# The mixture-of-experts part of a diffusion trunk: another order for the program of experts with 97 to 160 tokens

## The chip, the cores and the metric

The kernel runs on one core of a Trainium2 chip. The core has a matrix engine (PE; PEld is its loading of stationary weights), a vector engine (DVE), a scalar engine (ACT), a general engine (POOL) and an engine that only starts transfers (SP); sixteen DMA engines move data between the main memory and the core. Each engine runs its own queue of instructions in order, and they wait for each other by semaphores. The metric is the device time of one execution in microseconds; several runs are taken and their median is given.

## What is computed

One layer of a trunk: a mixing part (projections, convolutions, two recurrent scans) and then a mixture of 32 experts over 256 tokens of width 1024. The change touches the experts alone. Cut to these, the reference is:

```python
def moe_ffn(h, w_router, b_router, w_gate, b_gate, w_up, b_up, w_down, b_down):
    t = h.reshape(-1, shape[-1])                      # 256 x 1024
    logits = t @ w_router + b_router
    top_logit, top_idx = lax.top_k(logits, 4)         # 4 of 32 experts for each token
    top_w = softmax(top_logit)
    combine = ...                                     # expert x token, zero where not chosen
    def expert(acc, prm):
        gate = minimum(t @ wg + bg, 7)
        up = clip(t @ wu + bu, -7, 7)
        y = ((up + 1) * gate * sigmoid(1.702 * gate)) @ wd + bd
        return acc + cw[:, None] * y, None
```

All is float32. The three weight matrices of an expert have 4 MB each, so 384 MB are read in all.

## The kernel before

**Routing.** The number of tokens of each expert is known only when the kernel runs. For each expert the kernel holds five programs and branches to one by the count: up to 32 tokens (the light one), up to 64, up to 96, up to 160, and more. Every program is a list of groups (`SIZES`): a group is a start and a width in the expert's list of tokens. The program for 97 to 160 has three groups: 32 wide from 0, 64 wide from 32, 64 wide from 96. The five programs stand in the code once for each of the 32 experts.

**Gather and one-hots.** `pick` builds a one-hot matrix, tokens by places of the list, by comparing each token's rank in the expert with the place (DVE or POOL). `gather` multiplies the tokens' rows by it on PE, into the bank `xb`, and ACT copies them out. The first 96 places of an expert are gathered ahead, during the expert before; places from 96 on are gathered at the start of its own program. `to_slots` turns a one-hot by two transposes on PE, also into `xb`, and ACT copies it to SBUF (`ST`, `STm`): the turned form is needed to scatter.

**Products.** The weights of an expert are twelve tiles of 1 MB: four for gate, four for up, four for down. `some(prod, i, j)` multiplies group j by tile i: the tokens are PE's stationary operand, the weights stream. A 32-wide group uses a quarter of the columns of the array, so that four parts of the output are computed side by side; a 64-wide one uses a half. The result lies in one PSUM bank (`bk`): two single banks `g0` and `g1` and four banks of one tile `four`. ACT copies it out (`copy`), PE turns it (`fold`, into the bank `fb`), and DVE and ACT make the gate from it (`gated`) or the hidden activation (`up`). `copy` targets are `sA`, `sB`, `sC` and here also `gts[3]`; `gts[j]` holds the gate of group j.

**The ring.** The weights lie in a ring of 16 places of 1 MB. When the last group of an expert has used tile i, `fetch` issues the load of the tile 16 further on, on SP's queue. The loads wait for their place to come free.

**Scatter.** `scatter` multiplies the turned one-hot with the down product of a group (`spread`, into all of `four`) and DVE adds the result, weighted, to `acc` in two instructions (`rows` in the profile). The program of two groups spreads both groups in one accumulation and adds once.

**The order.** The schedule is written out by hand: each engine gets its instructions in the order of the source. For three groups the branch `else` of `program` is taken before the change: gather of the last group; all gate products; copy and gate of each group in turn; all up products; then turning of the first one-hot, copy and fold of each group; gather of the first half of the next expert's tokens; down products; gather of the second half; and for each group by itself a turned one-hot and a scatter. Groups 1 and 2 share the copy target `sC` there.

Of the kernel before, what the change touches and what calls it, by code (L numbers as in the profile page):

```python
# [198 lines left out]
def trunk(ctx: ExitStack, tc: tile.TileContext, I, out, offs, dbg=None, nexp=NE):  # L199
    nc = tc.nc  # L200
    V, S_, P_, G_ = nc.vector, nc.scalar, nc.tensor, nc.gpsimd
# [37 lines left out]
    def t512(name, dt=F32):  # L239
        return tp.tile([128, 512], dt, tag="f2", name=name)  # L240
# [1391 lines left out]
    rs, nb = rn[:, 0:2], rn[:, 2:4]  # L1632
# [83 lines left out]
    def etile(name, *shape):  # L1716
        return ep.tile([128, *shape], F32, name=name)
# [5 lines left out]
    Xm = [etile(f"Xm{i}", n) for i, n in enumerate((512, 512, 256))]  # L1723
    SMm, ST, STm = etile("SMm", 2, 128), etile("ST", T), etile("STm", T)
    gts = [t512(f"gt{i}") for i in range(4)] + [etile("gt4", 256)]
    sA, sB = (etile(n, 512) for n in ("sA", "sB"))
    scr = st.tile([128, 2, 512], F32, tag="hl", name="scr")
    sC, sg = scr[:, 0], scr[:, 1]
# [16 lines left out]
    def gather(Sm, X, n, ks=range(8)):  # L1745

        for k in ks:
            o = (k - ks[0]) * n
            for t in range(2):
                P_.matmul(xb[:, o:o + n], hl[:, t, k * 128:(k + 1) * 128], Sm[:, t, 0:n],  # L1750
                          start=(k == ks[0] and t == 0), stop=(t == 1), skip_group_check=True)
        S_.activation(X[:, ks[0] * n:(ks[-1] + 1) * n], xb[:, 0:len(ks) * n], AF.Copy)  # L1752

    def to_slots(Sm, st_, half=0):

        o = 256 * half
        for t in range(2):
            P_.transpose(xb[:, o + t * 128:o + (t + 1) * 128], Sm[:, t], ident)  # L1758
        S_.activation(st_, xb[:, o:o + 256], AF.Copy)

    def product(ps, e, i, x, n):

        w = raw(e, i)
        m = 8 * n
        for kk in range(2):
            k = 2 * (i % 4) + kk
            for q in range(128 // n):
                P_.matmul(ps[n * q:n * q + n, 0:m], x(k), w[:, kk * 1024 + q * m:kk * 1024 + (q + 1) * m],  # L1768
                          start=(k == 0), stop=(k == 7), skip_group_check=True)
# [5 lines left out]
    def chs(ap, n):  # L1775

        return ap.rearrange("p (c q s) -> p c q s", c=n // 16, s=n)
# [29 lines left out]
    def spread(parts):  # L1807

        for j, (st_, Y, n) in enumerate(parts):
            for t in range(2):  # L1810
                for i in range(n // 32):
                    for q in range(128 // n):
                        b = n // 32 * q + i
                        P_.matmul(four[:, b, t * 256:(t + 1) * 256], st_[n * q:n * q + n, t * 128:(t + 1) * 128],  # L1814
                                  Y[n * q:n * q + n, i * 256:(i + 1) * 256], start=(not j and not t), stop=(j == len(parts) - 1),
                                  skip_group_check=True)
        return [four[:, :, t * 256:(t + 1) * 256] for t in range(2)]

    def scatter(e, parts):

        ps = spread(parts)
        for t in range(2):
            a = acc[:, t].rearrange("p (q m) -> p q m", m=256)
            V.scalar_tensor_tensor(a, ps[t], cw[:, t, e:e + 1], a, op0=OP.mult, op1=OP.add)  # L1824

    def program(e, groups, first=True):

        nb, nxt = len(groups), e + 1 < nexp
        X0, Xn = Xt[e % 2], Xt[1 - e % 2]
        mine = range(0 if first else 1, nb)  # L1830
        ns = [n for a, n in groups]

        Hs = ([X0[:, 0:8 * ns[0]], X0[:, 256:768]] + Xm)[:nb]

        def x(j):
            a, n = groups[j]
            if a < 96:
                X = X0.rearrange("p (k s) -> p k s", s=96)
                return lambda k: X[:, k, a:a + n]
            X = Hs[j].rearrange("p (k s) -> p k s", s=n)  # L1840
            return lambda k: X[:, k]

        def bk(prod, j):
            return banks[(prod * nb + j) % 6]

        def v(ap, j):
            return chs(ap[:, 0:8 * ns[j]], ns[j])

        def some(prod, i, j):
            n = ns[j]  # L1850
            product(bk(prod, j), e, i, hid(v(Hs[j], j), n) if prod == 2 else x(j), n)
            if j == nb - 1:
                fetch(12 * e + i + NP)

        def gated(j, s):
            gate(e, fold(s, ns[j]), ns[j], v(gts[j], j), v(sg, j))

        def up(j, s):
            hidden(e, fold(s, ns[j]), ns[j], v(gts[j], j), v(Hs[j], j))

        def copy(prod, j, s):
            return copied(bk(prod, j), s, ns[j])

        def onehot(j):
            a, n = groups[j]
            return Sq[e % 2] if (a, n) == (0, 32) else pick(e, a, n, 128 // n, SMm, V)

        hint(e + 1)
        if nb == 1:
            for i in range(4):  # L1870
                some(0, i, 0)
            copy(0, 0, sA)
            for i in range(4, 7):
                some(1, i, 0)
            gated(0, sA)
            some(1, 7, 0)
            copy(1, 0, sB)
            if first:
                to_slots(onehot(0), ST)
            up(0, sB)  # L1880
        elif nb == 2:
            Sm = onehot(1)
            for j, s in enumerate((sA, sC)):
                for i in range(4):
                    some(0, i, j)
                copy(0, j, s)
            gated(0, sA)
            for i in range(4, 8):
                some(1, i, 0)
            copy(1, 0, sB)  # L1890
            gated(1, sC)
            for i in range(4, 8):
                some(1, i, 1)
            copy(1, 1, sC)
            up(0, sB)
            if first:
                to_slots(onehot(0), ST)
            to_slots(Sm, STm, 1)
            up(1, sC)
        else:  # L1900
            for j in range(2, nb):
                gather(onehot(j), Hs[j], ns[j])
            for j in range(nb):
                for i in range(4):
                    some(0, i, j)
            for j in range(nb):
                copy(0, j, sC if j else sA)
                gated(j, sC if j else sA)
            for j in range(nb):
                for i in range(4, 8):  # L1910
                    some(1, i, j)
            if first:
                to_slots(onehot(0), ST)
            for j in range(nb):
                copy(1, j, sC if j else sB)
                up(j, sC if j else sB)
        if nxt:
            gather(Sg[1 - e % 2], Xn, 96, range(4))
        if not mine:
            return  # L1920
        if nb == 1:
            for i in range(8, 12):
                some(2, i, 0)
        else:
            for j in mine:
                for i in range(8, 12):
                    some(2, i, j)
        parts = []
        for j, y in zip(mine, (sA, sB, sC, sg, gts[0])):
            parts.append((j, copy(2, j, y), ns[j]))  # L1930
        if nxt:
            gather(Sg[1 - e % 2], Xn, 96, range(4, 8))
        if nb <= 2:
            scatter(e, [(STm if j else ST, y, n) for j, y, n in parts])
        else:
            for j, y, n in parts:
                if j:
                    to_slots(onehot(j), STm)
                scatter(e, [(STm if j else ST, y, n)])
# [111 lines left out]
    for t in range(2):  # L2051
        V.tensor_tensor(xres[:, t], xres[:, t], rows[:, 0], op=OP.mult)
        V.tensor_tensor(xres[:, t], xres[:, t], rows[:, 1], op=OP.add)
    G_.memset(acc, 0.0)
    for e in range(nexp):
        last = e == nexp - 1
        if not last:
            known(e + 1)
            picked(e + 1, G_)
        else:  # L2060
            to_slots(Sq[e % 2], ST)
        if e in (20, 21):
            next(bd_)
        with tc.If(which[e] > 32, label=f"heavy{e}") as light:
            with tc.If(which[e] <= 64) as more:
                program(e, SIZES[2 if last else 3], not last)
            with more.Else():
                with tc.If(which[e] <= 96) as more:
                    program(e, SIZES[2], not last)
                with more.Else():  # L2070
                    with tc.If(which[e] <= 160) as more:
                        program(e, SIZES[1], not last)
                    with more.Else():
                        program(e, SIZES[0], not last)
        with light.Else():
            program(e, SIZES[4], not last)
# [28 lines left out]
```

## Time and profile before

| | |
|---|---|
| median of 3 runs | 1443.89 us (1442.87 to 1446.61) |
| profiled execution | 1443.94 us |
| its span, first to last instruction | 1442.0 us |
| PE busy | 1150.8 us (80%) |
| DVE, ACT, POOL busy | 489.6, 297.6, 192.5 us |
| read from main memory | 456.45 MB, 317 GB/s over the span |

Times of rows are microseconds from the start of the span. A row of the timeline is a run of like instructions on one engine: when it starts, how long it lasts, the line, what it writes and reads, how many; in brackets how long the engine stood idle before it and what ended that. "issue" is idle time for which the profile shows no wait. A float32 product is two instructions on PE. [...]

### The profile page before, as it was taken

What the parts mean: (1) busy time and instruction counts of PE and PEld (TensorE: products, weight loads), DVE (VectorE), ACT (ScalarE), POOL (GpSimd) and SP (SyncE); (2) the same over time, 40 slices, a digit from 0 to 9 for tenths busy, and PEclk for the clock granted to TensorE, in tenths of its full rate; (3) what the DMA queues carried; (4) which work ended last, traced back from release to release, by engine and by line L of the source; (5) the groups of instructions that cost most, each with busy time, mean ns of one, the idle gap of its engine ahead of it and who ended that gap; (6) DMA issues with size and microseconds to landing.
All of it is one profiled execution on the core that took longest, in us unless ns stands there. A gap on an engine that the chain in (4) does not pass through costs nothing.

```text
span 1442.0 us, 26141 instructions
## 1 busy us (share of the span) xinstructions
PE 1150.8 (80%) x11226; PEld 708.8 (49%) x11226; DVE 489.6 (34%) x863; ACT 297.6 (21%) x576; POOL 192.5 (13%) x229
## 2 busy tenths in 40 slices
PE   6797999899697897787787988686677869767783
PEld 1576888678444544354333643353333434433342
DVE  3767767979511211212022211121121112211116
ACT  3456644444210111111010101010001001101012
POOL 0242243450200100010000100010000101000002
PEclk9998979999698998998797989898879989898997
DMA  7634334418796998999943999999999999999970
GB/s 286 239 110 131 111 117 148 175 67 317 317 419 262 417 420 357 418 416 417 385 159 129 412 419 418 417 418 416 419 412 419 408 408 420 405 417 418 416 287 30
DMA packets 129059, 460.59 MB, mean 319 GB/s; under 512 B 9488, under 2 KB 19088, under 8 KB 128048
## 3 DMA queue, kind: packets, MB, share of 16 engines
q1 hardware_dynamic: 128816, 457.52, 79.8%
q8 instruction: 131, 2.15, 0.6%
q14 instruction: 112, 0.92, 0.2%
HBM read 456.45 MB, written 1.05 MB: 317 GB/s over the span
## 4 chain that ended last, share of the span: by engine, by line
PE 54%; DMA 22%; DVE 11%; issue 8%; ACT 4%; SPq 1%; DVEq 0%; ACTq 0%
PE g L1768 18%; PE four L1768 11%; DMA ring<-in_w_down 11%; DMA ring<-in_w_up 6%; PE xb L1750 6%; PE four L1814 3%; DMA ring<-in_w_gate 2%; PE fb L1786 2%; DMA bd<-in_b_down 1%; DMA uada<-in_w_ada 1%; PE psada L429 1%; DVE gt L1794 1%; PE psW L1005 1%; ACT scr L1796 1%; SPq L266 1%
## 5 line engine op out<-in xcount | busy, mean ns | idle before, releaser
L1768 PE MATMUL g<-ring,X 128*32 128x256 f32 (+1 forms) x3680 | 355.9, 472 | 142.2 <-issue 87.5
L1768 PEld LDWEIGHTS g<-ring,X 128*32 128x32 f32 (+1 forms) x3680 | 157.2, 128 | 320.2 <-issue 233.8
L1768 PE MATMUL four<-ring,X 128*32 128x256 f32 (+1 forms) x2272 | 208.6, 435 | 20.3 <-DMA ring<-in_w_down 19.6
L1824 DVE SCALAR_TENSOR_TENSOR rows<-four,cw,rows 128x1024 f32<-128x1024 f32 x66 | 81.7, 1280 | 329.6 <-PE four L1814 329.6
L1794 DVE TENSOR_TENSOR gt<-fb,vc 128x256 f32<-128x256 f32 (+1 forms) x37 | 18.7, 504 | 423.7 <-PE fb L1786 423.7
L1768 PEld LDWEIGHTS four<-ring,X 128*32 128x32 f32 (+1 forms) x2272 | 86.0, 118 | 123.5 <-issue 60.9
L1750 PE MATMUL xb<-Sg,hl 128*128 128x96 f32 x1024 | 135.4, 288 | 4.5 <-DVE Sg L1736 2.6
L1750 PEld LDWEIGHTS xb<-Sg,hl 128*128 128x128 f32 x1024 | 125.6, 200 | 27.2 <-issue 24.6
L1736 POOL TENSOR_SCALAR Sq<-slots,rank 128x128 f32<-128x128 f32 x62 | 39.4, 647 | 580.8 <-PE xb L1758 342.2
L1772 ACT ACTIVATE sA<-g 128x256 f32<-128x256 f32 (+1 forms) x33 | 14.0, 423 | 342.5 <-PE g L1768 342.5
L645 POOL TENSOR_TENSOR adas<-adas,uada 128x1024 f32<-128x1024 f32 x24 | 59.8, 2492 | 99.3 <-ACT uada L643 98.9
L1736 POOL TENSOR_SCALAR Sg<-slots,rank 128x96 f32<-128x96 f32 x62 | 31.6, 521 | 301.1 <-PE xb L1750 257.3
L1752 ACT ACTIVATE X<-xb 128x384 f32<-128x384 f32 x64 | 31.4, 491 | 123.4 <-PE xb L1750 117.9
L1796 ACT ACTIVATE scr<-gt 128x256 f32<-128x256 f32 (+1 forms) x37 | 17.7, 480 | 172.8 <-DVE gt L1795 172.8
L1772 ACT ACTIVATE sA<-four 128x256 f32<-128x256 f32 (+1 forms) x30 | 12.8, 427 | 163.1 <-PE four L1768 163.1
L1814 PE MATMUL four<-sA,ST 32*128 32x256 f32 (+1 forms) x512 | 42.7, 406 | 1.6 <-DVE sA L1985 1.6
L643 ACT ACTIVATE uada<-uada,sT 128x1024 f32<-128x1024 f32 x32 | 35.7, 1140 | 9.4 <-DMA uada<-in_w_ada 9.2
L1802 DVE TENSOR_TENSOR X<-fb,vc 128x256 f32<-128x256 f32 (+1 forms) x36 | 18.0, 499 | 54.2 <-PE fb L1786 54.2
L1005 PEld LDWEIGHTS <-before 64*64 64x64 f16 x1088 | 29.8, 115 | 9.8 <-issue 3.8
L1814 PEld LDWEIGHTS four<-sA,ST 32*128 32x128 f32 (+1 forms) x512 | 28.1, 188 | 6.5 <-DVE sA L1985 2.1
L1797 DVE TENSOR_TENSOR gt<-gt,scr 128x256 f32<-128x256 f32 (+1 forms) x37 | 18.9, 510 | 20.5 <-ACT scr L1796 20.5
L1768 PE MATMUL four<-ring,Xm 128*64 128x512 f32 x96 | 21.1, 592 | 0.0
(560 smaller groups left out, 1558.0 us busy)
## 6 DMA issues: line engine op xcount, KB each, us to landing
ring<-in_w_gate SPq DMA_DIRECT2D x128, 1024.0 KB, 18.1
ring<-in_w_up SPq DMA_DIRECT2D x128, 1024.0 KB, 17.8
ring<-in_w_down SPq DMA_DIRECT2D x128, 1024.0 KB, 18.1
uada<-in_w_ada SPq DMA_DIRECT2D x24, 1024.0 KB, 5.3
uout<-in_w_out SPq DMA_DIRECT2D x4, 1024.0 KB, 5.2
uE<-in_w_in SPq DMA_DIRECT2D x2, 1024.0 KB, 5.5
uF<-in_w_in SPq DMA_DIRECT2D x4, 512.0 KB, 4.0
uG<-in_w_in SPq DMA_DIRECT2D x2, 1024.0 KB, 5.3
```

What stands on the lines that cost most here:

```text
L643: S_.activation(u[:, kk], u[:, kk], AF.Copy, scale=sT3[:, 2 * h + kk, 0:1])
L645: G_.tensor_tensor(acc_, acc_, u[:, kk], op=OP.add)
L1005: P_.matmul(ps[cs, x * 64:x * 64 + 64], L[cs, x], R[cs, x] if len(R.shape) == 3 else R[cs], start=True, stop=True, skip_group_check=True)
L1736: eng.tensor_scalar(Sm[:, t, 0:m * n].rearrange("p (q s) -> p q s", s=n), slots[:, a:a + n].unsqueeze(1).to_broadcast([128, m, n]), rank[: ...
L1750: P_.matmul(xb[:, o:o + n], hl[:, t, k * 128:(k + 1) * 128], Sm[:, t, 0:n], start=(k == ks[0] and t == 0), stop=(t == 1), skip_group_check ...
L1752: S_.activation(X[:, ks[0] * n:(ks[-1] + 1) * n], xb[:, 0:len(ks) * n], AF.Copy)
L1768: P_.matmul(ps[n * q:n * q + n, 0:m], x(k), w[:, kk * 1024 + q * m:kk * 1024 + (q + 1) * m], start=(k == 0), stop=(k == 7), skip_group_che ...
L1786: P_.transpose(fb[:, c * 128:(c + 1) * 128], s[:, c * 128:(c + 1) * 128], ident)
L1794: V.tensor_tensor(g, p, bias(Cv('bg'), e, n), op=OP.add)
L1796: S_.activation(sg, g, AF.Sigmoid, scale=1.702)
L1814: P_.matmul(four[:, b, t * 256:(t + 1) * 256], st_[n * q:n * q + n, t * 128:(t + 1) * 128], Y[n * q:n * q + n, i * 256:(i + 1) * 256], sta ...
L1824: V.scalar_tensor_tensor(a, ps[t], cw[:, t, e:e + 1], a, op0=OP.mult, op1=OP.add)
```

## The change

The branch for two groups becomes the one for two and three. With three, the last group is gathered and its one-hot turned at the start, into `Xm[2]`. The gate products of all three groups are made and copied as before, the third to `gts[3]`; then the gate of a group is folded ahead of the up products of the same group, so that its DVE and ACT steps run beside these. The last one-hot but one is turned where the first is. The scatter takes all three groups in one accumulation. Ahead of the loop over the experts, POOL clears eight columns of four tiles. The programs for one, two and five groups keep their order.

```diff
-        elif nb == 2:
+        elif nb <= 3:
+            if nb == 3:
+                Sm = onehot(2)
+                gather(Sm, Hs[2], 64)
+                to_slots(Sm, Xm[2])
             Sm = onehot(1)
-            for j, s in enumerate((sA, sC)):
+            for j, s in enumerate((sA, sC, gts[3])[:nb]):
                 for i in range(4):
                     some(0, i, j)
                 copy(0, j, s)
-            gated(0, sA)
-            for i in range(4, 8):
-                some(1, i, 0)
-            copy(1, 0, sB)
-            gated(1, sC)
-            for i in range(4, 8):
-                some(1, i, 1)
-            copy(1, 1, sC)
+            for j, (s, s2) in enumerate(((sA, sB), (sC, sC), (gts[3], gts[3]))[:nb]):
+                gated(j, s)
+                for i in range(4, 8):
+                    some(1, i, j)
+                copy(1, j, s2)
             up(0, sB)
             if first:
                 to_slots(onehot(0), ST)
             to_slots(Sm, STm, 1)
             up(1, sC)
+            if nb == 3:
+                up(2, gts[3])
         else:
...
-        if nb <= 2:
-            scatter(e, [(STm if j else ST, y, n) for j, y, n in parts])
+        if nb <= 3:
+            scatter(e, [((ST, STm, Xm[2])[j], y, n) for j, y, n in parts])
...
     G_.memset(acc, 0.0)
+    for i in range(4):
+        G_.memset(gts[i][:, 0:8], 0.0)
```

## Rows read from the trace of the kernel before

**Rows 1.** Windows of expert 10, and of all behind it; columns as told above.

```profile
678.49:691.59 13.10, 0.00 (x1) 0.03 (x1) 2.87 (x4) 0.00 (x0) 0.00 (x0) 0.69 1.03 410
717.03:723.47 6.44, 2.14 (x13) 1.33 (x11) 2.95 (x6) 2.02 (x4) 0.00 (x0) 0.81 1.01 397
723.47:743.11 19.64, 19.64 (x130) 7.11 (x129) 1.81 (x3) 0.63 (x1) 0.00 (x0) 0.89 0.26 94
768.59:785.39 16.80, 10.06 (x53) 6.48 (x52) 5.73 (x8) 1.26 (x3) 1.02 (x2) 0.61 0.30 120
773.60:785.39 11.79, 8.25 (x34) 5.45 (x34) 2.87 (x4) 0.56 (x2) 1.02 (x2) 0.50 0.02 5
788.90:1380.00 591.10, 463.49 (x4464) 247.50 (x4468) 108.42 (x179) 61.90 (x142) 42.16 (x74) 0.89 1.02 413
```

**Rows 2.** Timeline of expert 10, PE and ACT: gather, first products, evacuation of the gather.

```profile
691.59 7.06 PE L1750 MATMUL xb<-SMm,hl 128*128 128x64 f32 x32 [13.10 <-issue]
698.58 1.94 PE L1768 MATMUL g<-ring,X 128*32 128x256 f32 x16
698.74 0.60 ACT L1752 ACTIVATE Xm<-xb 128x512 f32<-128x512 f32 x1 [20.80 <-PE xb L1750]
```

**Rows 3.** Timeline of expert 10, PE: second and third fold of the gate.

```profile
719.31 0.66 PE L1786 MATMUL fb<-cons,scr 128*128 128x128 f32 x4 [1.85 <-ACT scr L1772]
722.42 1.12 PE L1786 MATMUL fb<-cons,scr 128*128 128x128 f32 x4 [2.45 <-ACT scr L1772]
```

**Rows 4.** Timeline of expert 4 (two groups), PE: folds, then the scatter's products.

```profile
515.17 0.44 PE L1786 MATMUL fb<-cons,sA 128*128 128x128 f32 x2
519.13 0.66 PE L1786 MATMUL fb<-cons,scr 128*128 128x128 f32 x4
526.75 0.44 PE L1786 MATMUL fb<-cons,sB 128*128 128x128 f32 x2
543.37 1.15 PE L1814 MATMUL four<-sA,ST 32*128 32x256 f32 x16
544.44 2.00 PE L1814 MATMUL four<-sB,STm 64*128 64x256 f32 x16
```

**Rows 5.** Timeline, turning to gather: PE in expert 10; PE and DVE in expert 1.

```profile
743.11 0.44 PE L1758 MATMUL xb<-cons,Sq 128*128 128x128 f32 x2
747.31 1.92 PE L1750 MATMUL xb<-Sg,hl 128*128 128x96 f32 x16
...
432.38 0.44 PE L1786 MATMUL fb<-cons,sB 128*128 128x128 f32 x2
434.42 0.69 DVE L1802 TENSOR_TENSOR X<-fb,vc 128x512 f32<-128x512 f32 x1 [0.35 <-PE fb L1786]
434.51 2.00 PE L1750 MATMUL xb<-Sg,hl 128*128 128x96 f32 x16
```

**Rows 6.** Timeline of expert 10, PE: the three runs of scatter products.

```profile
768.59 1.15 PE L1814 MATMUL four<-sA,ST 32*128 32x256 f32 x16
773.83 3.78 PE L1814 MATMUL four<-sB,STm 64*128 64x256 f32 x16 [0.47 <-ACT STm L1759]
781.61 3.78 PE L1814 MATMUL four<-scr,STm 64*128 64x256 f32 x16 [0.53 <-ACT STm L1759]
```

**Rows 7.** Windows from PE's last product to the next expert's first: experts 1, 10, 15, 30.

```profile
452.08:459.64 7.56, 0.00 (x0) 0.03 (x1) 2.48 (x2) 0.00 (x0) 0.00 (x0) 0.68 0.27 103
785.39:788.90 3.51, 0.01 (x2) 0.03 (x2) 2.48 (x2) 0.00 (x0) 0.00 (x0) 0.92 0.03 7
919.56:929.47 9.91, 0.00 (x1) 0.03 (x1) 2.48 (x2) 0.00 (x0) 0.00 (x0) 0.65 1.03 412
1394.89:1399.87 4.98, 0.41 (x3) 0.23 (x3) 2.48 (x2) 0.38 (x1) 0.00 (x0) 1.00 0.08 27
```

**Rows 8.** Timeline, PE: first products of the light experts behind experts 1 and 10.

```profile
459.64 8.91 PE L1768 MATMUL g<-ring,X 128*32 128x256 f32 x112 [7.57 <-issue]
788.90 7.94 PE L1768 MATMUL g<-ring,X 128*32 128x256 f32 x112 [3.50 <-issue]
```

## Prediction

> **What bounds the kernel now.** I read in this order: the windows (which stretch is TensorE's and which is the DMA's), the timeline of the one stretch that the change rewrites, then the timelines of experts that already run in the new form.
>
> The three-group program runs once. Its mark is a gather into Xm, and one such gather stands in the timeline [rows 2]; a five-group expert would show three. It belongs to expert 10, from 691.59 us, when PE begins, to 785.39, when its last product ends. The other experts run the one-group and two-group programs, whose order the diff leaves as it was. So the change is worth what that one stretch is worth.
>
> In it PE sets the pace. The windows [rows 1] show the DMA at shares of 0.26 and 0.30 while the up products and the scatter run, and at 0.02 from 773.60 on: all 16 places of the ring are full and no load can be issued before PE uses one up. When expert 11 begins, at 788.90, loads start again, and from there to 1380 us the DMA share is 1.02. So everything behind 788.90 hangs on one moment, PE's first products of expert 11: whatever brings that forward moves the rest by the same amount. The last loads of the stretch follow its down products, so they move up with whatever is gained ahead of these; only what is gained behind them eats into the 15.3 us in which the DMA stands still.
>
> **The change part by part.** All against the profiled execution: 1443.94 us, of which 1442.0 are the span; the median of the three runs is 1443.89, so no correction is needed.
>
> *One-hots turned early.* Before, the gather is followed at once by the first products, at 698.58 [rows 2]. Now the third one-hot is turned there, on xb, the bank that the gather has just filled: PE must wait for ACT's evacuation (698.74 + 0.60 = 699.34) and then do two transposes, 0.44 at full clock [rows 5], some 0.7 at the half clock that is granted there (the first sixteen product instructions took 1.94 us). Products start at about 700.0: **1.4 lost**. Behind the wait stand all of PE's products. DVE's next pick (the second one-hot, into the same tile SMm) waits for the transposes, with nothing behind it before the first gate near 718. The clock rose to full soon after the first products; if it rises later by the wait or more, up to the 3.4 us that a 32-group takes at full clock is lost again. I take **1.0** of 0 to 3.4.
>
> *Folds of the gate under the products.* Before, PE goes from the first fold, at 717.03, to the turning at 743.11: 26.08 us. In it the second and third fold each wait for ACT's copy, which stands in ACT's queue behind a sigmoid [rows 3], and the idle time drops the granted clock to 0.81 in that stretch and to 0.89 under the products that follow [rows 1]. The new order is that of the two-group program, which ran in expert 4 at full clock [rows 4]: fold, 32-group, fold, 64-group took 526.75 - 515.17 = 11.58, and the last fold and 64-group of these 526.75 - 519.13 = 7.62. A third group adds another 7.62: 19.20. The copies now lie between products that write other banks of the same tile, four; if PE waits for each of two 0.60 us copies (the length in rows 2) beyond the fold that covers it, 0 to 1.0 is added, and I take 0.5. **Gain 26.08 - 19.7 = 6.4** (5.9 to 6.9). Copies, sigmoids and DVE's gate steps cost nothing here, since 7 us of products cover each group's.
>
> *Folds of the up products.* Before, turning to gather took 747.31 - 743.11 = 4.20. In the two-group program it takes 434.51 - 432.38 = 2.13, with both turnings in it [rows 5]. The third fold must wait until DVE has read fb, at 434.42 + 0.69 = 435.11, and takes some 0.66, as the earlier folds of its size: 435.8, so 3.4. **Gain 0.8** (0 to 1.4). The rest of DVE's work for the second and third group runs under the gather and the first down products.
>
> *One scatter.* Before, each group's products wait for DVE to add the last group's sums, to pick a one-hot anew, and for PE and ACT to turn it: 768.59 to 785.39, 16.80 us at a granted clock of 0.61 [rows 1]. Two of the three product runs take 3.78 each [rows 6]; the same instructions took 2.00 at full clock in expert 4, right behind the 32-group's [rows 4]. Now it is 32-group, 64-group, 64-group without a wait: 544.44 - 543.37 + 2.00 + 2.00 = 5.07. **Gain 11.7**; if the clock still fell, 1.15 + 3.78 + 3.78 = 8.7 and a gain of 8.1. DVE adds the sums once (2 instructions for 6), behind PE's last product, under the jump that follows.
>
> *The way out.* This is what the gains must pay. Behind a heavy program PE stands before the next one's first product: 3.51 us here, but 7.56 behind expert 1 and 9.91 behind expert 15, with the DMA share at 0.27 and 1.03 [rows 7]. [...] Experts 1 and 15 end without a wait, as expert 10 now will. The last loads then finish when PE does: they ended at 773.6, follow the down products, and move by 1.4 + 1.0 - 6.4 - 0.8 = -4.8, to 768.8; PE ends at 785.39 - 4.8 - 11.7 = 768.9. That is expert 1's case, where the loads also stop at the exit. I take its 7.56: **4.05 lost** (0 to 6.4). After it the first light products took 8.91 against 7.94 [rows 8]; half of that delays the first loads: **0.5 lost**.
>
> [...]
>
> *Moved or added at no cost.* Four memsets on POOL before the first expert: POOL's picks there are for the next expert, some 13 us ahead of their use. The order of SP's loads is unchanged, as each is still issued when the last group has used a place. PE's instruction count is the same (as many transposes, folds and products), DVE has six fewer.
>
> **Sum:** -1.4 - 1.0 + 6.4 + 0.8 + 11.7 - 4.05 - 0.5 = 11.95. 1443.94 - 11.95 = **1432.0 us**.
>
> **Rivals.**
> - *The jump stays hidden.* Exit 3.51 as before, and no later rise of the clock: -1.4 + 6.4 + 0.8 + 11.7 = 17.5, so 1426.4. For it: expert 30, with the DMA at 0.08, needs 4.98 with transposes in it [rows 7]. Against: expert 1.
> [...]
> [...]
> - *Slower: code reads at the other jumps.* The program is laid out 32 times, and its new length moves every jump's target. One heavy entry or exit can cost 6.4 more (9.91 against 3.51), and the entry of expert 10 already stands 13.10 us. Ten experts run heavy programs. Two such losses eat the 12; the third ends on the other side, 1443.94 - 12 + 19.2 = 1451. Against: PE's count of instructions hardly moves, and where the DMA is behind, a later PE costs nothing.
> - *It is handed back to the DMA.* Behind the down products at most 11.7 of the 15.3 us of idle DMA are used up, so the ring is full again in every case above; I give it no chance of its own.
>
> **How the numbers follow.** Forecast 0.62, jump hidden 0.16, dear exit 0.10, within 0.3% 0.07, slower 0.05. A measurement of this kernel can tell about 0.3% from no change, 4.3 us: faster 0.88, same 0.07, slower 0.05. The range reaches from the first rival (1426.4) to the dear exit (1437.2), with a little for the runs' spread: 1426 to 1437.5.
>
> **What would show it.** Gather to first products of expert 10 with an evacuation and two transposes between, some 1.4 us; first fold to turning 19.2 to 19.7 with the clock at full; one run of scatter products of 5.1 us; two instructions of DVE on rows instead of six; then a gap on PE of 5 to 8 us. Wrong would be: a half clock in the scatter, PE waiting for ACT before each up group, or a gap of 10. If PE's start of expert 11 moves by 12 us and the end does not, the claim that all behind it shifts is wrong.

## The result

The median of four executions is 1429.48 us (1423.75 to 1435.11) against 1444.01 before; the ratio is 0.9897, with a 95% interval of 0.9855 to 0.9938. Six further executions, in the first experiment, gave 1428.34. The forecast was 1432.0, from 1426.0 to 1437.5. The profiled execution took 1435.11 us, with a span of 1433.3. It is the slowest of the four, so its parts are compared, not its sum.

The windows of the changed kernel, for the same steps of expert 10 as in [rows 1] and [rows 7]. A row gives the stretch and its length, the busy time of PE, PEld, DVE, ACT and POOL, each with the count of its instructions, then the granted TensorE clock as a share of the full one, the busy share of the DMA engines and the rate in GB/s:

```profile
694.94:703.36 8.42, 7.68 (x35) 7.16 (x35) 0.11 (x1) 0.60 (x1) 0.00 (x0) 0.50 1.03 420
703.36:723.38 20.02, 20.02 (x129) 7.27 (x128) 0.39 (x2) 1.37 (x3) 0.00 (x0) 0.87 0.71 281
723.38:743.19 19.81, 19.32 (x140) 7.43 (x139) 4.77 (x9) 3.25 (x6) 0.00 (x0) 1.00 0.56 214
743.19:746.47 3.28, 2.02 (x16) 1.55 (x15) 2.31 (x6) 1.35 (x3) 0.00 (x0) 1.00 1.03 420
767.75:772.55 4.80, 4.80 (x49) 3.73 (x48) 0.00 (x0) 0.49 (x1) 1.02 (x2) 1.00 1.03 412
772.55:778.36 5.81, 0.01 (x1) 0.03 (x1) 2.47 (x2) 0.00 (x0) 0.00 (x0) 0.87 0.05 20
778.36:1369.50 591.14, 473.84 (x4472) 255.88 (x4476) 108.63 (x179) 62.05 (x142) 42.47 (x74) 0.87 1.02 413
```

Row by row these are: gather to first products; gate products; first fold to the end of the up products; up folds; scatter; the way out; all that follows. The scatter went from 16.80 us at a clock of 0.61 to 4.80 at 1.00, and the fold-and-up stretch from 26.08 (6.44 + 19.64 in [rows 1]) to 19.81 at 1.00. The last row is the one to hold against the last of [rows 1]. Its end was set so that both windows are equally long; what they show is the same DMA share, 1.02, and the same rate, 413 GB/s. So the stretch behind expert 10 runs at the old pace, started earlier.

From PE's first instruction of the gather to the first product of expert 11 it is 778.36 - 694.94 = 83.42 us, against 788.90 - 691.59 = 97.31: **13.9 gained**. The spans of the two profiled executions differ by less, 8.7: 3.35 is lost ahead of expert 10 and 1.9 behind it, in code that runs in the same order in both.

The timeline of the changed kernel, PE, ACT and DVE, shows the new order:

```profile
702.09 0.60 ACT L1752 ACTIVATE Xm<-xb 128x512 f32<-128x512 f32 x1 [20.81 <-PE xb L1750]
702.74 0.69 PE L1758 MATMUL xb<-cons,SMm 128*128 128x128 f32 x2 [0.74 <-ACT Xm L1752]
703.36 13.23 PE L1768 MATMUL g<-ring,X 128*32 128x256 f32 x96
...
724.20 3.66 PE L1768 MATMUL four<-ring,X 128*32 128x256 f32 x64 [0.38 <-ACT gt L1772]
727.79 0.66 PE L1786 MATMUL fb<-cons,scr 128*128 128x128 f32 x4
...
768.83 2.00 PE L1814 MATMUL four<-sB,STm 64*128 64x256 f32 x16
770.66 1.89 PE L1814 MATMUL four<-scr,Xm 64*128 64x256 f32 x16
772.68 2.47 DVE L1824 SCALAR_TENSOR_TENSOR rows<-four,cw,rows 128x1024 f32<-128x1024 f32 x2 [23.78 <-PE four L1814]
778.36 8.85 PE L1768 MATMUL g<-ring,X 128*32 128x256 f32 x112 [5.81 <-issue]
```

PE waits for the evacuation of the gather (0.74) and for ACT's copy out of `four` (0.38), and no longer for DVE or ACT between the parts of the scatter; the two 64-group runs take 2.00 and 1.89 us where [rows 6] have 3.78.

### The profile page after: what moved, and what is told of

Read it like the earlier page. It is cut to its first block, busy times and chain, and to the rows that moved or that the text cites. A ratio compares the mean times of both kernels' runs of the same rounds, so it can differ in the third digit from the quotient of the medians.

```text
span 1433.3 us, 26137 instructions
## 1 busy us (share of the span) xinstructions
PE 1156.2 (81%) x11226; PEld 713.9 (50%) x11226; DVE 485.9 (34%) x857; ACT 298.1 (21%) x576; POOL 191.0 (13%) x233
## 3 DMA queue, kind: packets, MB, share of 16 engines
q8 instruction: 131, 2.15, 0.6%
HBM read 456.45 MB, written 1.05 MB: 319 GB/s over the span
## 4 chain that ended last, share of the span: by engine, by line
PE 53%; DMA 24%; DVE 11%; issue 8%; ACT 4%; SPq 0%; DVEq 0%; ACTq 0%
PE g L1768 17%; DMA ring<-in_w_down 12%; PE four L1768 12%; DMA ring<-in_w_up 8%; PE xb L1750 6%; PE four L1814 2%; DMA ring<-in_w_gate 2%; PE fb L1786 2%; PE psada L429 1%; DMA bd<-in_b_down 1%; DMA uada<-in_w_ada 1%; PE psW L1005 1%; DVE gt L1794 1%; ACT scr L1796 1%; PE psada L438 1%
## 5 line engine op out<-in xcount | busy, mean ns | idle before, releaser
L1768 PE MATMUL g<-ring,X 128*32 128x256 f32 (+1 forms) x3680 | 350.1, 466 | 141.7 <-issue 89.0
L1768 PEld LDWEIGHTS g<-ring,X 128*32 128x32 f32 (+1 forms) x3680 | 153.8, 127 | 319.6 <-issue 228.6
L1824 DVE SCALAR_TENSOR_TENSOR rows<-four,cw,rows 128x1024 f32<-128x1024 f32 x62 | 76.7, 1279 | 339.9 <-PE four L1814 339.9
L1750 PEld LDWEIGHTS xb<-Sg,hl 128*128 128x128 f32 x1024 | 133.8, 211 | 29.2 <-issue 26.5
L1750 PE MATMUL xb<-Sg,hl 128*128 128x96 f32 x1024 | 143.9, 300 | 4.7 <-DVE Sg L1736 2.6
L1814 PE MATMUL four<-sA,ST 32*128 32x256 f32 (+1 forms) x512 | 46.5, 440 | 1.8 <-DVE sA L1988 1.8
L1786 PE MATMUL fb<-cons,sB 128*128 128x128 f32 x76 | 15.5, 300 | 7.4 <-ACT sB L1772 7.4
```

The source lines that it names most:

```text
L1786: P_.transpose(fb[:, c * 128:(c + 1) * 128], s[:, c * 128:(c + 1) * 128], ident)
```

## The experiments

How far a whole execution can be trusted is the first thing to know. The kernel before ranged from 1438.04 to 1452.85 us over the 23 executions that ran beside the first four experiments. In the profiled executions of all the kernels here the first product of expert 0, ahead of which nothing was edited but the place of code and four memsets on POOL, came between 377.7 and 389.2 us. So each experiment is read twice: by its times, and by the stretch of its own trace that the edit touches.

### The changed kernel again

> The changed kernel once more, unaltered. Its first four executions spread over 11 us (1423.75 to 1435.11), those of before over 4. If the spread is the TensorE clock's, which rises at another moment in each execution after PE has stood still, the mean granted clock of a run goes with its time and expert 10's own parts keep their lengths wherever the clock is full: first fold to fold of sB 19.8 us, scatter products 4.8. If the gain itself is unstable, one of these parts changes by several us at full clock. Median expected at 1429 to 1432, ratio about 0.990.

Measured: 1428.34 us (1423.44 to 1431.33), ratio 0.9888 (0.9855 to 0.9921). Gather to expert 11's first product took 83.00 us, against 83.42 the first time; fold to fold 19.81 again, the scatter again 4.80. The ten executions of the changed kernel thus spread over 12 us while the edited stretch differs by 0.4 between the two that were profiled: the spread comes from elsewhere. As the expectation asks, it goes with the mean granted clock: the three fastest of the ten executions (1423.44 to 1425.70 us) have 0.899 to 0.900, the three slowest (1430.02 to 1435.11) 0.876 to 0.887; of the 23 of the kernel before, the two fastest have 0.895 and 0.896, the two slowest 0.872 and 0.876. The gain holds.

### The third one-hot turned later

```diff
                 gather(Sm, Hs[2], 64)
-                to_slots(Sm, Xm[2])
-            Sm = onehot(1)
+            else:
+                Sm = onehot(1)
...
                     some(0, i, j)
                 copy(0, j, s)
+                if nb == 3 and j == 0:
+                    to_slots(Sm, Xm[2])
+                    Sm = onehot(1)
```

> As the changed kernel, but the third one-hot is turned after the 32-group's gate products and not right behind the gather. If the early turning cost what the trace says (1.4 us of waiting for the evacuation and transposing, and up to 3 us by a clock that rises later), gather to first products falls from 8.4 to 7.0 us, two transposes of 0.4 us and the switch to them appear between the 32-group and the next, and the time falls by 1 to 3 us against the changed kernel: 1427 to 1429 where that has 1430. The rival, that the wait is covered by something else which would then end last, expects no change.

Measured: 1427.70 us (1425.15 to 1432.89), ratio 0.9891 (0.9858 to 0.9924): not to be told from the changed kernel. In the trace the wait is gone, as expected: the first products start 6.99 us after the gather's start, not 8.42, and the two transposes cost 0.36 in the stream (timeline, PE):

```profile
687.21 7.06 PE L1750 MATMUL xb<-SMm,hl 128*128 128x64 f32 x32 [13.07 <-issue]
694.20 5.58 PE L1768 MATMUL g<-ring,X 128*32 128x256 f32 x64
699.71 0.44 PE L1758 MATMUL xb<-cons,SMm 128*128 128x128 f32 x2
700.07 7.09 PE L1768 MATMUL g<-ring,X 128*64 128x512 f32 x32
```

But gather to first fold of the gate is 26.75 us, against 27.15 in the run before and 28.44 in the first profile: 0.4 to 1.7 less, not 1.4 and up to 3 more. The first 32-group took 5.58 us where it takes 3.66 at full clock, as the granted clock was 0.50 in its first part. These are the windows from the start of the gather to the moment at which the clock rose: this kernel, the run before, and the first profile of the changed kernel. In each, PE was busy but for the one wait, and behind the window, up to the first fold, the clock is 1.00.

```profile
687.21:698.20 10.99, 10.99 (x72) 8.81 (x76) 0.00 (x0) 0.60 (x1) 0.00 (x0) 0.50 1.03 419
687.63:698.60 10.97, 10.23 (x58) 8.35 (x62) 0.50 (x2) 0.98 (x2) 0.00 (x0) 0.50 1.02 418
694.94:708.50 13.56, 12.82 (x85) 9.50 (x89) 0.50 (x2) 0.98 (x2) 0.00 (x0) 0.50 1.03 420
```

Against the run before, the products started 1.43 earlier and the clock rose at the same distance from the gather, so most of the wait had been paid for in time at half clock. But the two profiles of the changed kernel differ by 2.6 in that distance, more than the wait itself. The direction was right; the size is under what the times can show.

### The two parts one by one

The folds alone: the new order of folds and up products, the old scatter with a one-hot picked and turned for each group.

```diff
-                to_slots(Sm, Xm[2])
-            Sm = onehot(1)
+            else:
+                Sm = onehot(1)
...
-            to_slots(Sm, STm, 1)
+            if nb == 2:
+                to_slots(Sm, STm, 1)
...
-        if nb <= 3:
+        if nb <= 2:
             scatter(e, ...)
```

> The folds of the changed kernel with the three scatters of the kernel before (each with its own one-hot picked and turned anew; no turning behind the gather). By the prediction's terms: 6.3 gained at the gate, 0.9 at the up folds less the second turning, a scatter as before at 16.8 us and with it the short exit of 3.5: 7 gained, 1437. The rival, that only the shorter scatter matters and the folds are covered, expects 1444.

The scatter alone: the kernel before, with the third one-hot turned behind the gather, the second beside the first, and one scatter.

```diff
-                gather(onehot(j), Hs[j], ns[j])
+                Sm = onehot(j)
+                gather(Sm, Hs[j], ns[j])
+            if nb == 3:
+                to_slots(Sm, Xm[2])
+                Sm = onehot(1)
             for j in range(nb):
                 for i in range(4):
                     some(0, i, j)
...
                 to_slots(onehot(0), ST)
+            if nb == 3:
+                to_slots(Sm, STm, 1)
...
-        if nb <= 2:
+        if nb <= 3:
             scatter(e, ...)
```

> The scatter of the changed kernel (all three groups in one accumulation, the third one-hot turned behind the gather) with the order of gate and up folds of the kernel before. By the prediction's terms: 12 gained in the scatter, 1.4 to 3 lost at the early turning, 2.3 to 4 lost at a longer exit, some 0.4 for the second turning in the up stage: 5 to 8 gained, 1436 to 1439. If the two parts add up, its gain and that of the folds alone make the whole gain of 14.

Measured: folds alone 1438.31 us, ratio 0.9955 (0.9931 to 0.9979); scatter alone 1437.92, ratio 0.9955 (0.993 to 0.998). Both are gains, each about as put. The windows of the folds alone (fold to the end of the up products; scatter; way out):

```profile
722.62:742.42 19.80, 19.32 (x140) 7.46 (x138) 4.77 (x9) 3.25 (x6) 0.00 (x0) 1.00 0.55 219
766.66:782.98 16.32, 9.57 (x53) 6.36 (x52) 5.73 (x8) 1.26 (x3) 1.02 (x2) 0.76 0.32 129
782.98:786.99 4.01, 0.00 (x0) 0.03 (x1) 2.48 (x2) 0.00 (x0) 0.00 (x0) 0.50 0.03 6
```

And of the scatter alone (first fold to the turning; turning and up folds; scatter; way out):

```profile
721.86:746.72 24.86, 20.56 (x141) 8.03 (x139) 4.76 (x9) 2.65 (x5) 0.00 (x0) 0.93 0.44 164
746.72:752.24 5.52, 2.81 (x17) 1.92 (x15) 2.79 (x6) 2.13 (x5) 0.00 (x0) 0.86 1.02 406
776.04:780.84 4.80, 4.80 (x49) 3.73 (x48) 0.00 (x0) 0.49 (x1) 1.02 (x2) 1.00 1.02 410
780.84:787.11 6.27, 0.01 (x2) 0.04 (x2) 2.48 (x2) 0.00 (x0) 0.00 (x0) 0.82 0.07 25
```

Each part has the length in its kernel that it has in the whole change: 19.80 and 4.80. Over the whole stretch the folds gain 97.31 - 90.48 = 6.8 and the scatter 97.31 - 93.03 = 4.3, in sum 11.1 of the 13.9. Of the missing 2.8, 2.5 lie in the scatter alone, behind its up folds: PE stands still there as before, the granted clock is 0.86 over that window, the fold at 751.36 takes 1.09 us where the one of its size before it takes 0.63, the next gather takes 3.57 us where it takes 1.92 in the whole change, and from its start to the scatter it is 23.80 us against 21.28. So in these profiles the parts help each other through the clock. That the clock must fall there is not shown: in the kernel before, with nearly the same waits, it did not, and that gather took 1.92 [rows 5].

### More work in expert 10, and in expert 17

```diff
+        if nxt and nb == 3:            # in the other kernel: nb == 1 and e == 17
+            for _ in range(3):
+                gather(Sg[1 - e % 2], Xn, 96, range(4, 8))
```

> The changed kernel with the gather of the second half of the next expert's tokens done three times more in the three-group program, ahead of the scatter: some 2.7 us each, 8.0 in all, in which PE works and waits for the evacuation. If all behind expert 10 hangs on PE's first product of expert 11, the last loads keep their distance to that product and the time rises by 8: 1436 to 1438. If the DMA hides it, it stays at 1429. It also parts the causes of the longer way out: the loads now end some 7 us before PE's last product of expert 10, while the last 32 product instructions still have no wait ahead of them. If the loads' tail made the gap of 5.8 to 6.8 us, it falls to 3.5; if the missing wait made it, it stays at about 6.

> The same three gathers more, but in the light program of expert 17, where PE waits for loads (the DMA share there is 1.02). If PE's time costs nothing where the DMA is behind, the time stays at 1428 to 1430 and the DMA share behind expert 17 stays at 1.02; if PE's order sets the pace there too, it rises by 8 to 1437.

Measured: more in expert 10, 1433.43 us (1429.22 to 1435.72), 5 above the changed kernel, not 8; more in expert 17, 1420.49 us (1418.18 to 1421.87), **8 under it**, which no theory had. These two ran apart from the changed kernel. By the ratios to the kernel before, each beside its own executions of it, they are 0.9942 (0.9914 to 0.997) and 0.9848 (0.9819 to 0.9877) against 0.9888 (0.9855 to 0.9921), which is 7.8 above and 5.8 under. So the times give the signs; the sizes must come from the traces.

The stretches tell what the sums hide. In expert 10 the three gathers make the stretch 89.21 us, 6.2 above 83.00, and the end follows: from expert 11's first product it is 653.5 us to the end of the span, against 653.3. That is what "all behind expert 10 hangs on PE" asks for. The sum grew by less because 2.9 was gained ahead of expert 10 (303.9 us from expert 0's first product to the gather, against 306.8): the gap into expert 10 had shrunk by 5.4 and the one into expert 4 by 5.1, while the one into expert 1 had grown by 5.4. Into expert 10 (timeline, PE; the changed kernel again, then the one with more work in expert 10):

```profile
687.63 7.06 PE L1750 MATMUL xb<-SMm,hl 128*128 128x64 f32 x32 [13.13 <-issue]
```

```profile
684.62 7.06 PE L1750 MATMUL xb<-SMm,hl 128*128 128x64 f32 x32 [7.69 <-issue]
```

In expert 17 the added work cost nothing: in the window from the added gathers on, the DMA is as busy as ever (window of this kernel):

```profile
952.00:1300.00 348.00, 260.53 (x2554) 141.72 (x2552) 62.92 (x99) 35.32 (x81) 26.14 (x46) 0.90 1.02 414
```

From expert 11's first product to the end of the span it is 650.7 us in this kernel, against 653.3. Something was gained behind expert 17, and one gap differs: ahead of expert 30, PE stands 5.7 to 5.8 us in every kernel so far, and 0.3 to 0.4 in these two. What they share is that code was added ahead of expert 30, so that everything behind it lies elsewhere. That is a new theory, and two more kernels test it.

It can't be worth the whole gap. With more work in expert 17, expert 30 begins 5.7 earlier behind expert 11 than in the changed kernel again, and 3.1 of that is lost again by the end. With more work in expert 10 all of it is lost: PE stands a second time behind the first eight product instructions (timeline, PE).

```profile
1330.83 0.64 PE L1768 MATMUL g<-ring,X 128*32 128x256 f32 x8 [0.31 <-issue]
1335.82 12.48 PE L1768 MATMUL g<-ring,X 128*32 128x256 f32 x88 [4.35 <-issue]
```

### A wait ahead of the last products

```diff
+        if nb == 3:
+            for _ in range(4):
+                S_.activation(sg, sC, AF.Copy)
+                S_.activation(sC, sg, AF.Copy)
         if nb <= 3:
             scatter(e, ...)
```

> The changed kernel with eight copies more on ACT ahead of the scatter, between sC and sg and back, so that the last 32 product instructions wait for sC, by some 3 us. If a wait ahead of so few instructions lets the jump behind them be read early, the gap from PE's last product to expert 11's first falls from 6 to 3.5 us and takes back most of the 3 us: 1429 to 1431. If not, the gap stays at 6 and the time rises by 3: 1432.

Measured: 1428.75 us (1427.39 to 1430.06), as low as was expected for a hidden jump, but expert 10's stretch is 84.86 us against 83.00. In the trace the wait is there and the gap stays (timeline, PE, last run; windows: scatter, way out; the first pair is this kernel, the second the one with more work in expert 10):

```profile
763.60 2.00 PE L1814 MATMUL four<-scr,Xm 64*128 64x256 f32 x16 [2.72 <-ACT scr L1939]
```

```profile
757.80:765.60 7.80, 5.07 (x49) 3.65 (x48) 0.00 (x0) 5.42 (x9) 1.02 (x2) 1.00 0.74 286
765.60:771.17 5.57, 0.00 (x0) 0.03 (x1) 2.48 (x2) 0.00 (x0) 0.00 (x0) 0.80 0.03 7
```

```profile
763.88:768.68 4.80, 4.80 (x49) 3.73 (x48) 0.00 (x0) 0.49 (x1) 1.02 (x2) 1.00 0.04 10
768.68:773.83 5.15, 0.00 (x1) 0.03 (x1) 2.48 (x2) 0.00 (x0) 0.00 (x0) 0.99 0.03 6
```

With the wait 5.57; without a wait, but with the loads long ended, 5.15; without either, 5.81 and 6.67. So neither a wait nor early loads alone made the old 3.51. A wait and loads long ended together, as the kernel before has them, were not tried with a fast last run. What the kernels agree on better is the time from the **start** of the last run of products (x16 in the rows) to expert 11's first product: 7.29 us before, 7.70 and 8.57 in the changed kernel, 7.80 with the folds alone, 8.16 with the scatter alone, 7.57 here, 7.04 with more work in expert 10, 7.84 to 8.68 in the four others. What differs by more is the length of that last run: 3.78 at half clock before and 3.79 with the folds alone, 1.89 to 2.00 in the others. By this reading the way to the next expert runs from the start of the last run, beside it, and the slow run covered more of it.

These times spread by 1.6, and no kernel was made for this reading, but the traces have a sharper case of it, on the way from expert 9 into expert 10. There the changed kernel ran the last products once at half clock and once at full (timeline, PE; the first profile, then the second):

```profile
680.68 2.09 PE L1814 MATMUL four<-sA,ST 32*128 32x256 f32 x16
694.94 7.06 PE L1750 MATMUL xb<-SMm,hl 128*128 128x64 f32 x32 [12.17 <-issue]
```

```profile
673.35 1.15 PE L1814 MATMUL four<-sA,ST 32*128 32x256 f32 x16
687.63 7.06 PE L1750 MATMUL xb<-SMm,hl 128*128 128x64 f32 x32 [13.13 <-issue]
```

The gaps differ by 0.96 and the runs by 0.94; from the start of the run it is 14.26 and 14.28 us, and 14.2 to 14.3 in all nine profiles with a gap of 12 or 13.

### Nothing altered but the place of code

```diff
+        if nb == 5:                    # runs for no expert here
+            for _ in range({17: 6}.get(e, 0)):
+                gather(Sg[1 - e % 2], Xn, 96, range(4, 8))
```

> The changed kernel with 192 PE instructions more in the five-group program of expert 17, which no token count here reaches: nothing that runs is altered, only where the code behind expert 17 lies. Expert 30 then begins at the same place in PE's code as in the kernel with more gathers in expert 17 (which put the same 192 instructions there, in two programs), where the gap into expert 30 was 0.35 us against 5.7 to 5.8 in all kernels of the old layout. If the place of the code made that gap, it is 0.35 here too and the time is 4 to 6 under the changed kernel's: 1422 to 1424. If the added work did it, the gap stays at 5.8 and the time at 1428.

Measured: 1423.22 us (1420.77 to 1425.25), ratio 0.9871 (0.9848 to 0.9894): 5 under the changed kernel by the medians, as the theory of the place said, but only 2.5 by the ratios, whose intervals overlap. The first products of expert 30, in the changed kernel and in this one (timeline, PE):

```profile
1340.74 4.54 PE L1768 MATMUL g<-ring,X 128*32 128x256 f32 x56 [5.72 <-issue]
```

```profile
1324.10 1.93 PE L1768 MATMUL g<-ring,X 128*32 128x256 f32 x32 [0.34 <-issue]
1327.25 0.63 PE L1768 MATMUL g<-ring,X 128*32 128x256 f32 x6 [1.22 <-DMA ring<-in_w_gate]
1329.23 10.32 PE L1768 MATMUL g<-ring,X 128*32 128x256 f32 x58 [1.35 <-issue]
```

The instructions that PE executes are the same, and the gap is 5.4 us shorter: the place of the code makes it. But PE now stands twice more behind it, so that 0.34 + 1.22 + 1.35 = 2.91 us replace 5.78. From expert 11's first product to the end of the span it is 651.7 us, against 655.0 and 653.3 in the two profiles of the changed kernel: 1.6 to 3.3 of the 5 are there. The rest of what parts this profile from the second of the changed kernel lies ahead of expert 10, where no code had moved (expert 0's first product comes 2.2 earlier, and from there to expert 10 it is 1.6 less), and is not the edit's.

The second kernel takes the later turning and puts code that never runs at two places, 128 PE instructions at expert 2 and 64 at expert 5:

```diff
+            for _ in range({2: 4, 5: 2}.get(e, 0)):
```

That is 192 ahead of expert 30, as many as in the first of these two kernels, which has 0.34 there. The 0.7 and 7.7 us put for experts 4 and 10 are the gaps of the kernel with more work in expert 10 (0.73 and 7.69); that these amounts bring the two experts to like places was an estimate of the author's.

> [...] If the place of the code makes the gaps, into 4, 10 and 30 they are 0.7, 7.7 and 0.35 us. The loads still need their time at expert 4, so that gap gives 2 at most; with 5 at each of the others some 12 under the late turning's 1427.7: 1415 to 1419. If it doesn't, 1428.

Measured: 1412.82 us (1409.62 to 1416.18), ratio 0.98 (0.9775 to 0.9825), the fastest here and some 15 us under the changed kernel. The gaps into experts 4 and 10 are those that were named (timeline, PE; the first is 5.77 in the changed kernel, the second 12.17), into 30 it is 0.34:

```profile
491.30 2.37 PE L1768 MATMUL g<-ring,X 128*32 128x256 f32 x40 [0.37 <-issue]
...
674.71 7.06 PE L1750 MATMUL xb<-SMm,hl 128*128 128x64 f32 x32 [7.54 <-issue]
```

The time is under the 1415 to 1419 expected. By the trace expert 10's gather begins 297.0 us behind expert 0's first product, against 303.9 in the kernel with the later turning alone, from which the 7 had been counted: 6.9 were gained there, as put. Behind expert 11's first product it is 650.5 us against 653.6, 3.1 less, where 5 had been put. What remains of the difference of the two profiled executions, 5.6 of 15.7, is an earlier first product of expert 0 (377.7 against 383.3), in code that was not edited. The gap into expert 4 was not tried by itself.

## Why the prediction was right, step by step

- **What bounds the kernel: right.** Behind expert 10 the DMA share is 1.02 before and after, and from expert 11's first product to the end of the span it is 653.1 us before and 650.5 to 655.0 in the ten other profiles, while that product moved by over 30 us. Work added in expert 10 went through to the end, work added in expert 17 did not.
- **One-hots turned early: right.** 1.4 was put for the wait and 8.42 - 6.99 = 1.43 is there. For the clock 1.0 was put; the gate products took 20.02 us instead of 18.45, 1.6 more, in the first profile, and 18.73, 0.3 more, in the second. That 1.0 lies between them is luck, as the same kernel gave both. The later turning shows that the two don't simply add.
- **Folds of the gate: right.** 19.7 was put, 19.81 measured, with both of the small waits for ACT's copies that the tile `four` makes (0.38 in the row above; ahead of the third group's products 0.76 from its fold, where the second group has 0.60). The two-group program of expert 4 was the right model [rows 4].
- **Folds of the up products: right.** 3.4 put, 3.28 measured.
- **One scatter: right in size** (5.07 put, 4.80 measured), and by the cause given: no wait, so the clock holds at 1.00; the folds alone, with the waits, have 0.76 there.
- **The way out: wrong in its cause and too dear.** 4.05 was put, 2.3 came in the first profile and 3.2 in the second. That a wait of PE's just ahead of its last instructions, as the 0.53 for STm in [rows 6], keeps the way out short was the author's estimate. The kernel with such a wait has 5.57, so the wait alone does not do it. What [rows 6] and [rows 7] held, read together, is that the old gap was short because the last run was long: 781.61 + 7.29 = 788.90. By that reading 1.9 of the 11.7 that the scatter was to gain, the shortening of its last run, never was a gain, and the loss at the way out is mostly this same 1.9 given back. The rest, 0.4 to 1.3, is not settled: the same kernel has 7.70 and 8.57. The two cases without it (7.04 and 7.57 from the last run's start) had their loads ended earlier, which fits with the loads' tail. The rival of the hidden jump (3.51 as before, 1426.4) did not come true either: 5.81 and 6.67 lie nearer to the 7.56 put. Nor did a way out like expert 15's 9.91 (the dear exit) or a half clock in the scatter (within 0.3%), where 1.00 was granted.
- **First light products:** 0.5 was put for a slower start; they took 8.85 us against 7.94 in the first profile and 7.76 in the second, so the difference is one between executions, not of the change. The clock fits: it was 0.50 for 5.2 us of them in the first profile and for some 3.2 in the second.
- **The sum:** 11.95 put; 13.9 in the stretch, less 0.9 for the light products. Of the difference of 1.05 the way out is 1.75 and the scatter 0.3; the early turning (3.0 lost for 2.4 put) and the light products take back 1.0. That the median came so near 1432.0 is in part that these errors have opposite signs.
- **The rival of code reads at other jumps** did not come true for this change: the gaps into experts 1, 4 and 30 are 0.62, 5.77 and 5.72 us where they were 0.41, 5.96 and 5.83. Such gaps can turn, as the last two kernels show, but the change moves code by about four instructions for each expert (119 ahead of expert 30), and none of these did.

## What to carry to other kernels

Where one engine's standing still stops the loads too, price an edit by that engine's timeline alone, and take the new order's length from a place in the same trace that already runs in it. Judge the end of a program from the start of its last run of instructions, not from their end: on the way into expert 10 the next program began 14.26 and 14.28 us behind the start of runs of 2.09 and 1.15 us, so the 0.94 by which the run got shorter gained nothing there. And when an edit's sum disagrees with its own stretch, look at stretches that were not edited before looking for a cause in the edit.

## What was not expected of the hardware

**The place of code moves PE's standing by whole microseconds.** The gap ahead of a program of two groups was 0.3 to 1.1 or 5.7 to 6.0 us, and ahead of that of three groups 7.5 to 7.7 or 12.2 to 13.2, and one kernel altered nothing but where the code lay. For the same place it came back within 0.3 us, but for the two of 12.2, which followed a last run at half clock. A short gap is not all gain: in every program of two groups that had one, PE stood again, for 1.4 to 4.4 us, behind its first 8 to 41 product instructions, and where the gap was long it did not. Nor does what is saved all reach the end, as expert 30 shows: of the 5.4 us by which its gap got shorter, 1.6 to 3.3 are there, and ahead of it the DMA share is 1.02 (1200 to 1329 us in the changed kernel). The programs for 33 to 64 tokens, which stand first behind the outer branch, began without any such gap (experts 6, 14, 23 and 25, in all eleven profiles; in the one of before 1.07 to 1.10 us behind the start of a last run of 1.15, and 2.02 behind one of 2.09); that of two groups stands one inner branch further on, that of three two, and the kernel marks the outer branch alone for PE (`hint`). No kernel here was made to part these.

The profile of before counts instruction reads: queue q8 has 131 of them with 2.15 MB, 16 KB each. That such reads make the gaps is an estimate of the author's: the gaps come and go with the place of the code, by some 5.4 us, but no trace here ties a read to a gap. Which places are good was not settled.

**Executions of one kernel differ by ten microseconds** in parts that were not edited, as the first product of expert 0 at 377.7 to 389.2 us. For the kernel before and the changed one the time goes with the mean granted clock, as told above; in the four to six executions of each of the kernels from the one with more work in expert 10 on it does not show. What moves the clock was not tried.
